# Planning durations of a recorded program order: measured instruction lengths and a length for mode changes

## The chip, the cores and the metric

One core of one Trainium2 chip runs the whole program. The metric is the device time of one execution in microseconds (us); less is better. TensorE does the matmuls, VectorE (DVE), ScalarE (ACT) and GpSimd (POOL) the rest, SyncE (SP) issues most DMAs. Each engine takes its instructions in the order of the program and waits, in place, for what each of them needs.

## What is computed

One layer of a hybrid decoder on 512 prompt tokens and 8 x 4 sample tokens, all fp32, followed by a norm. Cut to what matters:

```python
h = rmsnorm(x, p['norm1_g'])
z = h @ p['w_in']                              # 1024 -> 74 * 128 columns
uz, vz, sz, qz, gz = _split(z, (D_A, D_A, P_SHIFT, D_C, N_BRANCH * D_MODEL))
vn = layernorm(jax.nn.gelu(vz), p['ln_v_g'], p['ln_v_b'])
y_a = u * spatial_gate(vn, p['sg_w'], p['sg_b'])
y_b, wkv_new = rwkv7_branch(rz, kz, vbz, wl, al, gl, wkv_prev, p)   # a recurrence over tokens
y_c = memory_cross_attn(qz, mk, mv)
proj = jnp.einsum('nbtc,ncd->nbtd', branches, p['w_branch'])
x = x + jnp.einsum('nbtd,btnd->btd', proj, gates) @ p['w_out']
x = x + jnp.square(jax.nn.relu(rmsnorm(x, p['norm2_g']) @ p['w_up'])) @ p['w_down']
```

## The kernel before

**The trunk.** All weight products (`memk`, `memv`, `win`, `br`, `wout`, `up`, `down`) run in `trunk` (L500). Tokens are the 544 moving columns, in two halves of 256 and 288; a tile of 128 output columns takes 8 steps `kt`, and in each step three products of split operands (high x high, low x high, high x low, in the fast fp32 form), so 6 matmuls a step and 48 a tile. A tile of `win` is one of 74, so there are 3552 projection matmuls. A generator yields after each `kt`, so other streams can come between. Each half tile of weights (128 x 512) is loaded by SP, copied to its high part by ScalarE (L198, `whi`), and its low part is subtracted by VectorE (L211, `wlo`).

**The stages.** First the memory keys and values, beside the first norm. Then the RWKV stage, seven streams in order of priority: `chain_stream`, `inv_stream`, `fill_stream`, `prep_stream`, `out_stream`, `sample_stream`, and the trunk with `win`. Heads go in four groups of two pairs; `prep_pair` makes a pair's operands, `inv_stream` inverts triangular blocks (30 pairs of GpSimd instructions, L1010 and L1012, then a VectorE copy L1015), `fill` transposes (L977, copies L984 and L985), and `chain_stream` walks 16 chunks of 32 tokens, each step in three phases: matmuls C1 (L1067, L1069) and the copy Wt (L1072) with four scaled copies SP (L1077); C2 (L1083) with the copies Xo, Xe (L1086, L1087) and YU (L1090); C3 (L1094, L1096) with the additions into the next chunk's Xe, Xo (L1102). Each phase ends with `yield DONE`. `out_stream` norms a group's outputs (L1113 to L1127), transposes, adds and gates them (L1144 to L1158, gate product L543) and stores them in `yb_d`. `sample_stream` does the sample tokens (L1189 to L1295, state products L1221 and L1273).

Then the attention stage: `yb_stream` loads `yb_d` (L1371) and splits it into high and low parts (L1379, L1381), after which the trunk may do the 24 tiles of `br`, first those of the RWKV branch; `gate_in` transposes the gate input (L1415, L1416), `layer_norm`, `gate_out` (L1494) and the two attentions follow. The sample attention multiplies 16 cache blocks (L1560). The last branch's tiles wait for both attentions. Last the MLP, nearly all trunk.

**What sets the order.** `body` runs twice. In the dry run the engines are `ModelEngine`s: each call goes to `Model.op`, which keeps for each engine the time at which it is free, and for each tile when and by which engine it was written. `Sched.run` resumes the first stream in the list that is ready by TensorE's planned time, and records the pick. After `NOW` a stream is ready at once, after `DONE` when the last result of its piece is there plus 0.22 us (`m.done + GAP`), after `AFTER(t)` and `PAUSE(t)` some time later. PSUM slots (`take`) are recorded too. The second run emits the instructions in the recorded order. No cost is in the program itself; it only sets who comes when. `SWITCH`, `tensor` and the durations in `op` are what the change touches.

Of the kernel before, what the change touches and what calls it, by code (L numbers as in the profile page):

```python
# [11 lines left out]
F32R = mybir.dt.float32r  # L12
AF = mybir.ActivationFunctionType
ALU = mybir.AluOpType
# [44 lines left out]
class Shape:  # L59


    def __init__(self, shape, dt, base=None):
        self.shape, self.dt = tuple(shape), dt
        self.base = base or self
        if base is None:
            self.wrote = (None, None, 0.0)
# [35 lines left out]
class Model:  # L102

    def __init__(self):
        self.free = {"pe": 0.0, "v": 0.0, "s": 0.0, "g": 0.0}
        self.piece, self.start, self.done, self.side = 0, 0.0, 0.0, False

    def begin(self, ready):  # L110
        self.piece += 1
        self.start = self.done = ready

    def op(self, eng, name, a, k):
        if name == "dma_start":
            if eng in ("g", "s"):
                self.free[eng] = max(self.free[eng], self.start) + (1.04 if eng == "g" else 0.1)
            return
        aps = [x for x in list(a) + list(k.values()) if isinstance(x, Shape)]
        n = max(math.prod(x.shape[1:]) for x in aps)  # L120
        out = k.get("out") or a[0]
        if eng == "pe":
            n = math.prod(out.shape[1:])
            r = 0.85e-3 if name == "transpose" else 0.424e-3 if aps[1].dt == F32R else 1.68e-3
            t = n * r
        elif eng == "g":
            t = 0.17 + n * 1.7e-3
        elif eng == "v":
            t = 0.07 + n / 960.0
        else:  # L130
            t = 0.06 + n / 1160.0
        b = max(self.free[eng], self.start)
        for x in aps:
            piece, by, at = x.base.wrote
            if piece == self.piece and by != eng:
                b = max(b, at + 0.2)
        self.free[eng] = b + t
        if not self.side:
            out.base.wrote = (self.piece, eng, b + t)
            self.done = max(self.done, b + t)  # L140


class ModelEngine:
# [201 lines left out]
def body(nc, tc, io, plan, dry, dbg=None):  # L345
# [92 lines left out]
    def affine(tl, pattern, op, base, mult):  # L438
        G.affine_select(out=tl, in_=tl, pattern=pattern, compare_op=op, fill=0.0, base=base, channel_multiplier=mult)
# [1580 lines left out]
```

## Time and profile before

| | us |
|---|---|
| median of 3 runs (1484.18 to 1491.03) | 1484.28 |
| the profiled execution | 1485.83 |
| its span, first to last instruction | 1484.1 |
| TensorE busy in the span | 1404.7 (95%) |
| VectorE, ScalarE, GpSimd busy | 908.4, 590.1, 395.8 |
| mean granted TensorE clock | 0.982 |

Times in the profile are microseconds from the span's start. L500 is line 500 of the kernel before; PE is TensorE, PEld its weight loads. A tile's buffer number is left out (`hh` stands for all eight). A matmul on plain fp32 operands shows as two records. "Granted clock" is the share of full speed (2.4 GHz) that the chip allowed TensorE; 0.5 is 1.2 GHz.

### The profile page before, as it was taken

The page shows a single profiled execution, that of the slowest core. Times are in us where ns is not written, and L with a number is a line of the kernel's source. Part 1 is how long each engine was busy: PE and PEld are TensorE (multiplying, and loading weights), DVE is VectorE, ACT ScalarE, POOL GpSimd, SP SyncE. Part 2 cuts the span into 40 slices and gives each one's busy share as a digit, 9 for nine tenths or more (in the row PEclk, how much of TensorE's full clock was granted, in tenths as well). Part 3 has the DMA queues.
Part 4 walks back from the last instruction along what each step waited for, and adds up shares of the span by engine and source line. Part 5 has one row for each costly group of instructions (what it writes and reads, how often), then busy time and mean ns, then how long its engine had stood idle before and what let it go on. Part 6 is the DMA issues. An engine that isn't in the chain of part 4 may idle for free.

```text
span 1484.1 us, 30949 instructions
## 1 busy us (share of the span) xinstructions
PE 1404.7 (95%) x12390; PEld 1303.5 (88%) x12390; DVE 908.4 (61%) x1586; ACT 590.1 (40%) x1476; POOL 395.8 (27%) x462
## 2 busy tenths in 40 slices
PE   7899998998999899999998999989999999999997
PEld 7899987887888788887888896769999999999996
DVE  5757777776878877577675753424664454444544
ACT  3434334555565365555434123212433423323222
POOL 5320191272106602730233430112100030120223
PEclk9899998999999999999999999999999999999998
DMA  6642221222322323243468657654423322323222
GB/s 210 176 139 82 91 72 63 70 67 75 108 73 65 104 83 98 78 146 109 130 198 280 224 170 240 200 193 125 138 86 93 93 86 86 94 83 95 87 86 83
DMA packets 101888, 177.43 MB, mean 120 GB/s; under 512 B 14928, under 2 KB 28496, under 8 KB 101744
## 3 DMA queue, kind: packets, MB, share of 16 engines
q1 hardware_dynamic: 99904, 172.06, 36.8%
q8 instruction: 98, 1.61, 0.5%
q0 software_dynamic: 640, 2.23, 0.4%
q10 hardware_dynamic: 1200, 1.16, 0.2%
q14 instruction: 46, 0.38, 0.1%
HBM read 147.89 MB, written 27.51 MB: 118 GB/s over the span
## 4 chain that ended last, share of the span: by engine, by line
PE 63%; DVE 7%; POOL 5%; DMA 3%; ACT 2%; issue 2%; SPq 1%; POOLq 0%; DVEq 0%; ACTq 0%
PE pst L500 51%; POOL Xinv L1012 2%; POOL Tt L1010 2%; PE psc L1083 1%; PE psc L1067 1%; DVE wlo L211 1%; PE psc L1094 1%; PE pst L1646 1%; PE pst L1679 1%; PE pst L543 1%; PE pst L1817 1%; DMA craw<-cv 1%; PE pst L923 1%; POOL gn_va L1126 1%; PE pst L1494 1%
## 5 line engine op out<-in xcount | busy, mean ns | idle before, releaser
L211 DVE TENSOR_TENSOR wlo<-wraw,whi 128x512 fp32r<-128x512 f32 x372 | 309.8, 851 | 54.3 <-ACT whi L198 51.7
L198 ACT CAST whi<-wraw 128x512 fp32r<-128x512 f32 x372 | 224.0, 618 | 175.1 <-PE pst L500 111.8
L500 PE MATMUL pst<-hh,whi 128*128 128x256 f32 (+1 forms) x1184 | 274.2, 313 | 9.1 <-DVE Em L985 4.5
L500 PE MATMUL pst<-hh,wlo 128*128 128x256 f32 (+1 forms) x1184 | 246.7, 290 | 2.3 <-DVE wlo L211 2.3
L500 PE MATMUL pst<-hl,whi 128*128 128x256 f32 (+1 forms) x1184 | 246.1, 289 | 0.0
L500 PEld LDWEIGHTS pst<-hh,whi 128*128 128x128 f32 x1184 | 188.4, 191 | 29.5 <-issue 10.2
L500 PEld LDWEIGHTS pst<-hh,wlo 128*128 128x128 f32 x1184 | 191.5, 190 | 2.7 <-DVE wlo L211 2.7
L500 PEld LDWEIGHTS pst<-hl,whi 128*128 128x128 f32 x1184 | 192.2, 191 | 0.0
L1785 POOL TENSOR_TENSOR x<-x,dn 128x544 f32<-128x544 f32 x24 | 41.7, 1737 | 292.8 <-DVE dn L1783 292.8
L500 PE MATMUL pst<-gh,whi 128*128 128x256 f32 (+1 forms) x512 | 106.2, 289 | 0.0
L500 PE MATMUL pst<-gl,whi 128*128 128x256 f32 (+1 forms) x512 | 105.5, 287 | 0.0
L500 PE MATMUL pst<-gh,wlo 128*128 128x256 f32 (+1 forms) x512 | 105.0, 287 | 0.0
L500 PE MATMUL pst<-y_h,whi 128*128 128x256 f32 (+1 forms) x384 | 83.7, 299 | 0.5 <-ACT y_h L1604 0.5
L500 PEld LDWEIGHTS pst<-gl,whi 128*128 128x128 f32 x512 | 82.7, 189 | 0.0
L1090 ACT COPY YU<-psc 32x64 f32<-32x64 f32 x256 | 51.9, 203 | 76.1 <-DVE Xe L1087 70.7
L500 PEld LDWEIGHTS pst<-gh,whi 128*128 128x128 f32 x512 | 81.9, 188 | 0.1
L500 PEld LDWEIGHTS pst<-gh,wlo 128*128 128x128 f32 x512 | 81.7, 188 | 0.0
L1010 POOL TENSOR_TENSOR Tt<-Xinv 128x30 f32<-128x30 f32 (+14 forms) x120 | 67.9, 566 | 45.9 <-DVE Xinv L1005 37.1
L500 PE MATMUL pst<-y_h,wlo 128*128 128x256 f32 (+1 forms) x384 | 79.6, 289 | 0.0
L500 PE MATMUL pst<-y_l,whi 128*128 128x256 f32 (+1 forms) x384 | 79.5, 288 | 0.0
L1012 POOL TENSOR_TENSOR Xinv<-Xinv,Tt 128x30 f32<-128x30 f32 (+14 forms) x120 | 75.2, 627 | 9.4
L500 PE MATMUL pst<-mh,whi 128*128 128x256 f32 (+1 forms) x256 | 66.4, 300 | 8.5 <-ACT whi L198 7.9
(399 smaller groups left out, 2913.0 us busy)
## 6 DMA issues: line engine op xcount, KB each, us to landing
wraw<-win SPq DMA_DIRECT2D x148, 256.0 KB, 2.9
wraw<-up SPq DMA_DIRECT2D x64, 256.0 KB, 2.9
wraw<-down SPq DMA_DIRECT2D x64, 256.0 KB, 2.9
wraw<-br SPq DMA_DIRECT2D x48, 256.0 KB, 3.4
craw<-ck SPq DMA_DIRECT2D x16, 512.0 KB, 5.4
craw<-cv SPq DMA_DIRECT2D x16, 512.0 KB, 4.5
gz_d<-gzs SPq DMA_DIRECT2D x24, 272.0 KB, 3.0
gt<-gz_d SPq DMA_DIRECT2D x24, 272.0 KB, 2.9
```

The costliest lines, as they stand in the source:

```text
L198: self.nc.scalar.copy(hi, raw)
L211: (self.nc.gpsimd if pool else self.nc.vector).tensor_tensor(lo, raw, hi, op=ALU.subtract)
L500: PE.matmul(ps[:, o:o + n], lhsT=w[:, c], rhs=x[kt][:, s:s + n], start=kt == 0 and i == 0, stop=kt == KT - 1 and i == 2)
L543: PE.matmul(ps[:, o:o + n], lhsT=lhsT, rhs=rhs[:, s:s + n], start=True, stop=True)
L923: PE.matmul(ps[64:128, o:o + 64], lhsT=BK[0:64, c, :], rhs=A2[0][0:64, pi, c, :], start=True, stop=True, tile_position=(0, 64))
L1010: G.tensor_tensor(t3, X[:, j + 1:32, j:j + 1].to_broadcast([128, n, j]), X[:, j:j + 1, 0:j].to_broadcast([128, n, j]), op=ALU.mult)
L1012: G.tensor_tensor(X[:, j + 1:32, 0:j], X[:, j + 1:32, 0:j], t3, op=ALU.add)
L1067: PE.matmul(ps[64:128, pi * 64:pi * 64 + 64], lhsT=Ae[0:96, pi, c, :], rhs=Xe[0:96, pi, c, :], start=True, stop=True, tile_position=(0, 64))
L1083: PE.matmul(ps[q:q + 64, pi * 64:pi * 64 + 64], lhsT=CT[q:q + 64, m, :], rhs=Wt[q:q + 64, pi, :], start=True, stop=True, tile_position=(q, q))
L1090: S.copy(YU[q + 32 * pi:q + 32 * pi + 32, c, :], p3[q:q + 32, pi, :])
L1094: PE.matmul(ps[0:64, pi * 64:pi * 64 + 64], lhsT=Em[64:128, pi, c, :], rhs=Xe[64:128, pi, c, :], start=True, stop=True, tile_position=(64, 0))
L1785: G.tensor_tensor(x1[j], x1[j], t, op=ALU.add)
```

## The change

The model's durations are replaced: each kind of instruction gets one of its own (a scaled copy on ScalarE 0.1 us more, a power on GpSimd 0.4 us and more, slower shared stretches of VectorE and GpSimd), the delay from a write to its reader on another engine is 0.27 us from TensorE and 0.12 us from others where it was 0.2 us, and TensorE's matmuls go through `tensor`, which knows three modes (r: fast fp32, the trunk; f: plain fp32; t: parts of the array) and adds `SWITCH` where the mode changes. Nothing else is edited. Lines behind it stand 36 further on in the changed kernel.

```diff
--- before.py
+++ after.py
@@ -103,13 +103,32 @@
 
 
 
+
     def __init__(self):
         self.free = {"pe": 0.0, "v": 0.0, "s": 0.0, "g": 0.0}
         self.piece, self.start, self.done, self.side = 0, 0.0, 0.0, False
+        self.mode = "r"
 
     def begin(self, ready):
         self.piece += 1
         self.start = self.done = ready
+
+    def tensor(self, name, out, aps, tiled):
+
+        n, m = math.prod(out.shape[1:]), math.prod(aps[1].shape[1:])
+        if name == "transpose":
+            t, mode = 0.109 * max(1.0, n / 128), "f"
+        elif aps[1].dt == F32R:
+            t, mode = 0.0125 + n / 2400, "r"
+        elif tiled:
+            at_once = 4 if m <= 32 and aps[1].shape[0] == 128 else 2
+            t, mode = 2 * (0.003 + n / (850 if aps[1].shape[0] == 64 and m == 128 else 1200)) / at_once, "t"
+        else:
+            t, mode = 2 * max(0.112, 0.0025 + n / 1200), "f"
+        if mode != self.mode:
+            t += SWITCH[self.mode + mode]
+            self.mode = mode
+        return t
 
     def op(self, eng, name, a, k):
         if name == "dma_start":
@@ -119,25 +138,42 @@
         aps = [x for x in list(a) + list(k.values()) if isinstance(x, Shape)]
         n = max(math.prod(x.shape[1:]) for x in aps)
         out = k.get("out") or a[0]
-        if eng == "pe":
-            n = math.prod(out.shape[1:])
-            r = 0.85e-3 if name == "transpose" else 0.424e-3 if aps[1].dt == F32R else 1.68e-3
-            t = n * r
-        elif eng == "g":
-            t = 0.17 + n * 1.7e-3
-        elif eng == "v":
-            t = 0.07 + n / 960.0
-        else:
-            t = 0.06 + n / 1160.0
         b = max(self.free[eng], self.start)
         for x in aps:
             piece, by, at = x.base.wrote
             if piece == self.piece and by != eng:
-                b = max(b, at + 0.2)
+                b = max(b, at + (0.27 if by == "pe" else 0.12))
+        if eng == "pe":
+            t = self.tensor(name, out, aps, "tile_position" in k or aps[1].shape[0] == 64)
+        elif eng == "g":
+            if k.get("op") == ALU.pow:
+                t = 0.4 + n * 0.17
+            elif name == "memset":
+                t = 0.09 + n * 0.9e-3
+            else:
+                t = 0.18 + n * (2.3e-3 if self.free["v"] > b else 1.7e-3)
+        elif eng == "v":
+            if name in ("memset", "tensor_scalar"):
+                t = 0.155 + n / 1920
+            elif name == "reciprocal":
+                t = 0.15 + n / 160
+            elif name == "tensor_tensor_scan":
+                t = 0.1 + n / 480
+            elif name == "transpose":
+                t = 0.17 + n / (960 if n < 1024 else 560)
+            else:
+                t = 0.155 + n / 960 * (1.25 if n >= 500 and self.free["g"] > b else 1.0)
+        else:
+            scaled = sum(isinstance(k.get(x), Shape) for x in ("scale", "bias"))
+            t = 0.17 + 0.1 * scaled + n / 1200
         self.free[eng] = b + t
         if not self.side:
             out.base.wrote = (self.piece, eng, b + t)
             self.done = max(self.done, b + t)
+
+
+
+SWITCH = {"rf": 0.0, "fr": 0.11, "rt": 0.09, "tr": 0.2, "ft": 0.1, "tf": 0.11}
 
 
 class ModelEngine:
```

The instructions are the same; their order is not. At TensorE before, at the end of the RWKV stage (the first four rows are phase C3 of a late chain step, L500 the trunk, L1273 a sample state product):

```order
L1094 MATMUL psc<-Xe,Em 64x64
L1096 MATMUL psc<-Xo,Em 64x64
L1094 MATMUL psc<-Xe,Em 64x64
L1096 MATMUL psc<-Xo,Em 64x64
L500 MATMUL pst<-hh_93,whi 128x256
L500 MATMUL pst<-hh_93,whi 128x288
L500 MATMUL pst<-hl_101,whi 128x256
L500 MATMUL pst<-hl_101,whi 128x288
L500 MATMUL pst<-hh_93,wlo 128x256
L500 MATMUL pst<-hh_93,wlo 128x288
L1273 MATMUL pst<-ux,Ebd 128x512
L1067 MATMUL psc<-Xe,AG1e 64x64
```

Now, at the same place (L1119 is C2, L1130 and L1132 C3, L1309 the state product, L579 the gate product of the last two pairs, L1451 a gate input's transposes; the trunk's line is L536):

```order
L1309 MATMUL pst<-ux,Ebd 128x512
L1119 MATMUL psc<-Wt,CT_1028 64x64 x4
L1130 MATMUL psc<-Xe,Em 64x64
L1132 MATMUL psc<-Xo,Em 64x64
L1130 MATMUL psc<-Xe,Em 64x64
L1132 MATMUL psc<-Xo,Em 64x64
L1309 MATMUL pst<-ux,Ebd 128x512 x2
L579 MATMUL pst<-lg,wg_10107 128x256
L579 MATMUL pst<-lg,wg_10107 128x288
L579 MATMUL pst<-lg,wg_10124 128x256
L579 MATMUL pst<-lg,wg_10124 128x288
L1451 MATMUL pst<-ident,gv 128x128 x4
```

Trunk rows stood between the phases and between the state products; now none stands between them, or between them and what follows.

At VectorE before, at the end of the first inversion (L1015 is the copy that follows it, L904 and L905 make a half of the operands AG of the next pair, L211 the weights' low part):

```order
L725 SCALAR_TENSOR_TENSOR t_v<-pst,vec,t_v 128x511
L727 SCALAR_TENSOR_TENSOR t_v<-pst,vec,t_v 128x8x3
L728 SCALAR_TENSOR_TENSOR t_v<-sst,vec,t_v 128x8
L211 TENSOR_TENSOR wlo<-wraw,whi 128x512
L1015 COPY Xinv<-qmask 128x32
L904 TENSOR_TENSOR AG1o<-t_r,PP 64x16x32
L905 SCALAR_TENSOR_TENSOR AG1o<-t_L,PP 64x16x32
L1017 STREAM_TRANSPOSE Tt<-Xinv 128x32x32
L211 TENSOR_TENSOR wlo<-wraw,whi 128x512
```

Now, at the same place (L1051 is that copy, L940 and L941 the operands AG, L247 the low part):

```order
L247 TENSOR_TENSOR wlo<-wraw,whi 128x512
L1051 COPY Xinv<-qmask 128x32
L940 TENSOR_TENSOR AG1e<-t_r,PP 64x16x32
L941 SCALAR_TENSOR_TENSOR AG1e<-t_L,PP 64x16x32
L1053 STREAM_TRANSPOSE Tt<-Xinv 128x32x32
L247 TENSOR_TENSOR wlo<-wraw,whi 128x512
L940 TENSOR_TENSOR AG1o<-t_r,PP 64x16x32
L941 SCALAR_TENSOR_TENSOR AG1o<-t_L,PP 64x16x32
```

The copy behind the inversion now stands ahead of both halves AG1e and AG1o, where it stood between them.

## Rows read from the trace of the kernel before

**Rows 1.** Windows by stage: us, then busy us of each engine, clock, DMA share, GB/s
```profile
105.00:740.00 635.00, 602.37 (x6216) 536.55 (x6216) 466.40 (x946) 329.31 (x984) 212.35 (x291) 0.98 0.28 89
...
812.00:988.00 176.00, 163.50 (x1235) 135.77 (x1233) 85.44 (x138) 41.56 (x96) 41.77 (x26) 0.98 0.63 209
988.00:1484.10 496.10, 485.15 (x3873) 484.05 (x3873) 242.66 (x325) 153.82 (x271) 76.89 (x54) 0.99 0.31 95
```

**Rows 2.** Chain that ended last, whole run: start us, us, what
```profile
230.94 3.09 PE pst L500 x12
245.17 1.70 PE pst L500 x12
...
1091.68 364.60 PE pst L500 x2922
```

**Rows 3.** TensorE's waits, 105 to 740 us: total us, times, longest
```profile
PE psc L1094 <- DVE Xe L1087: 5.2, 5, 2.9
PE pst L500 <- DVE Em L985: 4.5, 4, 1.4
PE psc L1067 <- DVE Xe L1102: 4.2, 4, 2.6
PE pst L925 <- DVE AG1o L905: 3.9, 1, 3.9
```

**Rows 4.** VectorE's waits, 105 to 740 us: one pair
```profile
DVE Xinv L1015 <- POOL Xinv L1012: 12.0, 4, 6.6
```

**Rows 5.** Windows, as rows 1: a stretch behind a wait; the crossing
```profile
225.00:236.00 11.00, 8.94 (x153) 8.33 (x154) 8.31 (x10) 1.99 (x4) 0.81 (x3) 0.53 0.23 74
...
739.40:812.00 72.60, 66.64 (x480) 62.73 (x479) 48.46 (x75) 25.16 (x52) 20.25 (x27) 0.98 0.75 251
```

**Rows 6.** Groups by form, 105 to 740 us: count, busy us, mean ns, idle before
```profile
L500 PE MATMUL pst<-hh,whi 128*128 128x256 f32 x500 | 165.4, 331 | 6.7 <-DVE Em L985 4.5 <-ACT CT L1029 1.3 <-DVE t_vb L914 0.9
...
L500 PE MATMUL pst<-hl,whi 128*128 128x256 f32 x500 | 140.7, 281 | 0.0
...
L1077 ACT ACTIVATE SP<-Xe,PC 64x64 f32<-64x64 f32 x120 | 35.3, 343 | 0.0
...
L1072 ACT COPY Wt<-psc 128x128 f32<-128x128 f32 x64 | 17.0, 266 | 54.3 <-PE psc L1069 53.7
...
L1102 DVE TENSOR_TENSOR Xe<-psc,SP 64x128 f32<-64x128 f32 x56 | 15.7, 281 | 22.6 <-PE psc L1096 19.8 <-ACT YU L1090 1.9
```

**Rows 7.** Chain that ended last, the crossing
```profile
741.87 0.86 PE pst L1273 x2
...
757.49 0.70 DVE y_f L1144
...
766.14 2.89 DMA yb_d<-y_f
```

**Rows 8.** VectorE in time: end of the chain (738 to 756), last split (788 to 800)
```profile
739.56 0.61 DVE L1102 TENSOR_TENSOR SF<-psc,SP 64x128 f32<-64x128 f32 x2 [1.67 <-ACT whi L198]
...
798.81 0.72 DVE L1381 TENSOR_TENSOR y_l<-ybs,y_h 128x544 fp32r<-128x544 f32 x1 [0.34 <-ACT y_h L1379]
```

**Rows 9.** GpSimd in time, the crossing: start us, us, instruction, idle before
```profile
749.08 2.90 POOL L1126 TENSOR_TENSOR gn_va<-gn_va,mhalf 128x16 f32<-128x16 f32 x1 [2.03 <-DVE gn_va L1124]
752.06 1.90 POOL L1127 TENSOR_TENSOR YU<-YU,gn_va 128x1024 f32<-128x1024 f32 x1
...
772.91 1.29 POOL L1152 TENSOR_TENSOR y_f<-y_f,vbr 128x512 f32<-128x512 f32 x1 [11.73 <-ACT y_f L1150]
782.21 1.31 POOL L1371 DMA_DIRECT2D ybs<-yb_d  x2 [8.02 <-DMA yb_d<-ysT]
```

**Rows 10.** The page, costliest groups: the inversion
```profile
L1010 POOL TENSOR_TENSOR Tt<-Xinv 128x30 f32<-128x30 f32 (+14 forms) x120 | 67.9, 566 | 45.9 <-DVE Xinv L1005 37.1
...
L1012 POOL TENSOR_TENSOR Xinv<-Xinv,Tt 128x30 f32<-128x30 f32 (+14 forms) x120 | 75.2, 627 | 9.4
```

**Rows 11.** TensorE's waits, 812 to 988 us: one pair
```profile
PE pst L1494 <- POOL sgw L439: 2.0, 1, 2.0
```

## The prediction

> **What bounds the kernel now.** I read the windows by stage first. TensorE is busy in 602.37 of the 635 us of the RWKV stage (105 to 740 us), in 163.50 of the 176 us from the first branch matmul on (812 to 988), and in 485.15 of 496.10 us behind that [rows 1]. So the kernel is a queue of TensorE work, and a change of order can only move idle time: that ahead of 105 us (where the first projection matmul waits for the first norm), some 33 us in the RWKV stage, 6 in the crossing to the branches, 12.5 in the attention stage. A dense trunk matmul costs 364.60 / 2922 = 0.125 us [rows 2].
>
> The waits of TensorE in the RWKV stage [rows 3] show who makes the 33 us: VectorE late with Xe (5.2 and 4.2 us) and with Em (4.5), the copies behind the fill transposes. VectorE itself was held four times, 12.0 us, by the triangular inversion on GpSimd [rows 4]. Then I read the crossing, 739.4 to 812 us: TensorE is busy in 66.64 of 72.60 us [rows 5], although the work there is a long dependent chain on other engines. Trunk matmuls cover it: after the last chain step the order of before still has 402 of the 3552 projection matmuls (counted in the order), 50 us of cover at 0.125. That cover is what the change touches.
>
> **The change part by part.** No instruction is added or removed; only the recorded picks, slots and placements differ. The number of TensorE's mode changes, counted in both orders, is 596 before and 596 now. Tile to trunk goes from 169 to 191, other fp32 to trunk from 97 to 81, tile to other fp32 from 39 to 26. Coming back to the trunk costs: the first matmul of a group means 331 ns where the like one in mid-group means 281 [rows 6], 50 ns over 500 matmuls, 25 us in all, some 0.1 us for each return. Twenty-odd returns of a dearer kind against thirty cheaper ones: 0 to 4 us, I take **+2**.
>
> *Chain spacing.* In a chain step Wt is copied in 266 ns, then four scaled copies SP of 343 ns follow on ScalarE [rows 6]. The second phase needs Wt alone, but the stream says DONE behind all five, and the planner resumes it after the last. The old costs made SP 0.115 us each, the new ones 0.32; so the planner now wants 18 trunk matmuls between phases one and two: counted over 64 steps, 18 stand there 32 times instead of 4 (12 stood there 41 times). Sixteen steps now stretch over 580 to 610 trunk matmuls where they took 410 to 520. At the end the difference falls due: in the order of before the last chain step has 402 projection matmuls behind it; now **none**. The projection runs out with 13 phases still to come, and the sample states, the last two gate products and all 40 gate-input transposes stand bare.
>
> *The bare phases.* Without filling a phase lasts about its copies (266 ns of Wt; two of Xe and Xo, two additions of 281 [rows 6]) with 0.5 us for the matmuls and hand-overs on either side: 1.0 to 1.3 us, so 13 take about 16 us. TensorE's work in them is about 11 us (six state products of 0.86 [rows 7], 13 chain groups at about half of one of those). Idle **+5**, bounds 2 and 10.
>
> *The bare crossing.* From the last state addition (739.56) to the last low part of the first branch input (end of 799.53) the chain takes 60 us [rows 8]. In it the group norm's last GpSimd steps take 2.90 and 1.90 us, and the loads of the branch input wait from 753.96 to 782.21 [rows 9]. Between 753.96 and 774.20 lie two pairs; each needs four transposes of 0.70, an addition of 1.29 and a like time for the rest, about 5.6 us, with a store of 2.89 between them [rows 7, 9]: 14 us of the 20. The other 6, and 2 more ahead of the norm, are VectorE work that trunk and samples bring; they leave with the trunk. So the crossing takes 52 us. TensorE's own work in it: 66.64 less 50 for the trunk, less some 7 that now stand earlier or later, 9 us. It idles 43 us instead of 6: **+37**, bounds 26 (a chain of 41 us) and 45 (all 60).
>
> *The clock.* After the 3.9 us wait for AG1o, at 221 us [rows 3], the granted clock was 0.53 from 225 to 236 us, the lower level for nearly all of it [rows 5], and twelve trunk matmuls took 3.09 us instead of 1.70 [rows 2]. The crossing will end the same way: **+3**, bounds 0 and 11. The Trainium skill, "TensorE: Matmul & The Clock Gate", section "HAM oscillation — how this bites in real kernels", says the same against this change: work that follows each long wait starts at half rate. By that the crossing's own TensorE work would all run at the lower level too, and the sum would be 8 us higher.
>
> *Waits inside the stage.* The better VectorE and TensorE costs spread the fills (the eight fill transposes of group 0 now stand over 144 trunk matmuls instead of 120), and chain phases have more room. I take 12 of the 33 us away, **-12**. Bounds: all 33, and nothing. I don't take more because the inversion stays under-costed: its 60 GpSimd instructions last (67.9 + 75.2) / 4 = 35.8 us [rows 10] where the new costs make 28 to 34 of them, and the copy that waits for them still stands 7 to 9 low-part subtractions behind the start, as before; in group 0 it even stands ahead of both AG pairs now. The 3.9 us wait for AG1o [rows 3] came from just that queue.
>
> *Attention stage.* The gate products now start 252 branch matmuls after the first instead of 204, so the 2.0 us wait for sgw [rows 11] goes: **-2**. The end of the stage is as before: branch work runs out with five cache products left in both orders. The MLP's order is the same but for three matmuls at the end. Stage 0 waits for its norm in either order: 0.
>
> Sum: 37 + 5 + 2 + 3 - 12 - 2 = +33 on the profiled 1485.83 us; that execution stands 1.55 above the median of 1484.28, so **1517 us**.
>
> **The rivals.**
> *The inversion holds more.* The copy behind it comes up sooner on VectorE, and weights' low parts queue behind it. If each of the four holds VectorE for its worst 6.6 us [rows 4] instead of 3.0, TensorE loses the most of 14 us and nothing is saved: 1517 + 12 + 12 = 1541 at worst, about 1532. For it: the place in group 0. Against: new costs add 1 to 6 us to the planned inversion.
> *A cold crossing.* The lower clock holds through the crossing, its 9 us double and the first branch matmuls run at half: 1517 + 8 = 1525, with a longer chain 1530. For it: the stretch at 0.53 [rows 5].
> *No change.* All 33 us of RWKV waits vanish while the crossing costs what I say: 1517 - 21 = 1496, and with the crossing at its lower bound 1485.
> *Faster.* The waits vanish in both planned stages, 33 + 12.5 us, and the inversion's with them, by costs that now fit the chip. Then 37 + 5 + 2 + 3 - 45.5 is +1.5; it is faster than before once the crossing idles under 34 us too, e.g. 28: 1476. Against it: what VectorE waits for is GpSimd and DMA, whose costs stay low.
>
> **How the numbers follow.** About 0.5%, 7.4 us, is what a measurement of this kernel can tell from no change. Forecast (1496 to 1525) 0.66; inversion 0.12; cold crossing 0.10; no change 0.08; faster 0.04. Slower by over 0.5% is the first three, 0.88; the same 0.08; faster 0.04. The range takes the forecast and most of the two dearer cases: 1494 to 1536.
>
> **What would show it.** In the profile after: projection matmuls end before the chain; TensorE under half busy for some 45 us ahead of the first branch matmul, at a granted clock well under 1; the mean C1-to-C2 distance longer, with fewer waits for Xe and Em; DVE Xinv waiting 10 us or more for GpSimd in all; the stretch from the first branch matmul to the end within 8 us of before's 672. The prediction is wrong if that bare stretch is under 25 us long, or if TensorE's waits in the RWKV stage fall by more than 30 us.

## The result: 1.6% slower, and the profile after

The changed kernel takes 1510.03 us (median of four runs, 1509.75 to 1510.31), the kernel before 1485.38 in the runs beside it: a ratio of 1.0158, 95% interval 1.0131 to 1.0185. The forecast was 1517 us, slower. The profiled execution of the changed kernel has a span of 1508.0 us against 1484.1 and a mean granted clock of 0.972 against 0.982. In its code everything behind the planner stands 36 lines lower: the trunk matmul L500 is L536, the state product L1273 is L1309, the inversion L1010/L1012 is L1046/L1048.

The windows of the changed kernel, cut where the same pieces of work end as in [rows 1, 5] (the last chain phase now ends at 791 us, the first branch matmul starts at 840.08):

```profile
105.00:740.00 635.00, 609.99 (x6129) 553.25 (x6127) 452.55 (x898) 318.92 (x927) 198.05 (x282) 0.99 0.30 93
740.00:791.00 51.00, 43.21 (x476) 31.39 (x476) 30.63 (x64) 21.58 (x77) 12.37 (x11) 0.87 0.30 97
791.00:840.00 49.00, 16.13 (x59) 10.36 (x60) 26.09 (x42) 11.40 (x28) 15.36 (x21) 0.57 0.55 179
840.00:1011.00 171.00, 164.44 (x1256) 138.71 (x1253) 92.76 (x147) 42.07 (x97) 43.38 (x28) 0.98 0.65 223
1011.00:1508.00 497.00, 485.73 (x3875) 484.45 (x3873) 243.21 (x326) 154.00 (x271) 77.02 (x54) 0.99 0.31 95
```

Read as idle time of TensorE (the stretch less its busy time) against [rows 1, 5], this is the whole difference. To 740 us 25.0 idle instead of 32.6, so 7.6 won. From there to the first branch matmul 7.8 + 32.9 = 40.7 instead of 6.0, so 34.7 lost. The branch stage 6.6 instead of 12.5, so 5.9 won. The rest 11.3 instead of 11.0; ahead of 105 us 17.6 instead of 17.3. Sum +21.8, and 2.1 more busy time (1406.84 instead of 1404.72): +23.9, which is 1508.0 less 1484.1.

What TensorE waits for between 740 and 850 us (total us, times, longest):

```profile
PE pst L579 <- DMA wg<-wg: 18.8, 2, 10.3
PE pst L1451 <- DMA gv<-zv_d: 13.2, 5, 7.7
PE psc L1130 <- DVE Xe L1123: 3.2, 4, 0.8
```

These are the two gate products and the transposes of the gate inputs, on an engine that has no projection matmul left: the last of those ends at 766.2 us. The named DMAs are only what ended last. The work ahead of them is the group norm and the store, the chain of [rows 8, 9]: SyncE issues the loads of the gate inputs behind the stores of that chain. From SyncE's queue, VectorE and TensorE in time:

```profile
819.47 0.32 SPq L1196 DMA_DIRECT2D yb_d<-y_f  x1
821.07 0.93 SPq L1440 DMA_DIRECT2D gv<-zv_d  x2
...
793.33 0.60 DVE L1138 TENSOR_TENSOR SF<-psc,SP 64x128 f32<-64x128 f32 x2
828.99 0.72 DVE L1417 TENSOR_TENSOR y_l<-ybs,y_h 128x544 fp32r<-128x544 f32 x1 [9.21 <-ACT y_h L1415]
840.00 0.72 DVE L1417 TENSOR_TENSOR y_l<-ybs,y_h 128x544 fp32r<-128x544 f32 x1 [0.23 <-ACT y_h L1415]
...
839.13 1.09 PE L1451 MATMUL pst<-ident,gv 128*128 128x128 f32 x4 [0.73 <-DMA gv<-zv_d]
840.08 0.80 PE L536 MATMUL pst<-y_h,whi 128*128 128x256 f32 x2
```

The first low part (y_l) is ready at 829.7 us, the last at 840.72. The first branch matmul at 840.08 follows the last gate-input transposes without a gap, so two things end the crossing together: the last split and, on TensorE, the transposes that the order puts ahead of the branch work.

### The profile page after: what moved, and what is told of

Same layout as the page of the kernel before. It is cut to its first block, busy times and chain, and to the rows that moved or that the text cites. A ratio compares the mean times of both kernels' runs of the same rounds, so it can differ in the third digit from the quotient of the medians.

```text
span 1508.0 us, 30958 instructions
## 1 busy us (share of the span) xinstructions
PE 1406.8 (93%) x12390; PEld 1301.0 (86%) x12390; DVE 910.2 (60%) x1586; ACT 590.1 (39%) x1476; POOL 392.0 (26%) x462
## 3 DMA queue, kind: packets, MB, share of 16 engines
q1 hardware_dynamic: 99904, 172.06, 35.9%
## 4 chain that ended last, share of the span: by engine, by line
PE 70%; DVE 10%; POOL 8%; DMA 5%; issue 4%; ACT 2%; SPq 0%; POOLq 0%; DVEq 0%; ACTq 0%
PE pst L536 57%; POOL Xinv L1048 4%; POOL Tt L1046 3%; DVE wlo L247 2%; PE pst L1715 1%; PE psc L1103 1%; PE pst L1682 1%; PE psc L1119 1%; PE psc L1130 1%; PE pst L579 1%; PE pst L959 1%; PE pst L1853 1%; DVE y_f L1182 1%; DVE y_f L1180 1%; DMA lng<-lng 1%
## 5 line engine op out<-in xcount | busy, mean ns | idle before, releaser
L247 DVE TENSOR_TENSOR wlo<-wraw,whi 128x512 fp32r<-128x512 f32 x372 | 315.1, 864 | 45.6 <-ACT whi L234 43.0
L536 PE MATMUL pst<-hh,whi 128*128 128x256 f32 (+1 forms) x1184 | 271.8, 311 | 11.5 <-DVE Em L1021 7.4
L536 PE MATMUL pst<-hh,wlo 128*128 128x256 f32 (+1 forms) x1184 | 245.9, 289 | 5.7 <-DVE wlo L247 5.7
L536 PE MATMUL pst<-hl,whi 128*128 128x256 f32 (+1 forms) x1184 | 244.5, 288 | 0.0
L536 PEld LDWEIGHTS pst<-hh,whi 128*128 128x128 f32 x1184 | 186.4, 189 | 33.4 <-issue 8.8
L536 PEld LDWEIGHTS pst<-hh,wlo 128*128 128x128 f32 x1184 | 190.3, 189 | 6.2 <-DVE wlo L247 6.2
L536 PEld LDWEIGHTS pst<-hl,whi 128*128 128x128 f32 x1184 | 190.3, 189 | 0.0
L536 PE MATMUL pst<-gh,whi 128*128 128x256 f32 (+1 forms) x512 | 106.2, 289 | 0.0
L536 PE MATMUL pst<-gl,whi 128*128 128x256 f32 (+1 forms) x512 | 105.5, 287 | 0.0
L536 PE MATMUL pst<-gh,wlo 128*128 128x256 f32 (+1 forms) x512 | 105.1, 287 | 0.0
L536 PE MATMUL pst<-y_h,whi 128*128 128x256 f32 (+1 forms) x384 | 84.6, 301 | 0.5 <-ACT y_h L1640 0.5
L536 PEld LDWEIGHTS pst<-gl,whi 128*128 128x128 f32 x512 | 82.7, 189 | 0.0
L536 PEld LDWEIGHTS pst<-gh,whi 128*128 128x128 f32 x512 | 81.9, 188 | 0.1
L536 PEld LDWEIGHTS pst<-gh,wlo 128*128 128x128 f32 x512 | 81.8, 188 | 0.0
L536 PE MATMUL pst<-y_h,wlo 128*128 128x256 f32 (+1 forms) x384 | 79.7, 289 | 0.0
L536 PE MATMUL pst<-y_l,whi 128*128 128x256 f32 (+1 forms) x384 | 79.3, 288 | 0.0
L1046 POOL TENSOR_TENSOR Tt<-Xinv 128x30 f32<-128x30 f32 (+14 forms) x120 | 66.9, 557 | 47.1 <-DVE Xinv L1041 38.3
L536 PE MATMUL pst<-mh,whi 128*128 128x256 f32 (+1 forms) x256 | 65.7, 297 | 10.5 <-ACT whi L234 8.1
L1048 POOL TENSOR_TENSOR Xinv<-Xinv,Tt 128x30 f32<-128x30 f32 (+14 forms) x120 | 72.5, 604 | 9.4
```

The costliest lines, as they stand in the source:

```text
L247: (self.nc.gpsimd if pool else self.nc.vector).tensor_tensor(lo, raw, hi, op=ALU.subtract)
L536: PE.matmul(ps[:, o:o + n], lhsT=w[:, c], rhs=x[kt][:, s:s + n], start=kt == 0 and i == 0, stop=kt == KT - 1 and i == 2)
L1046: G.tensor_tensor(t3, X[:, j + 1:32, j:j + 1].to_broadcast([128, n, j]), X[:, j:j + 1, 0:j].to_broadcast([128, n, j]), op=ALU.mult)
L1048: G.tensor_tensor(X[:, j + 1:32, 0:j], X[:, j + 1:32, 0:j], t3, op=ALU.add)
```

## The experiments

The planner spends trunk matmuls ahead of each chain phase until its model says that the phase's inputs are there. So each plan is described by three means (trunk matmuls between phases one and two, two and three, three and the next one) and by how many projection matmuls it leaves behind the chain; both are counted in the order. My first theory, the **cover theory**, was the prediction's step: time goes with what is left behind the chain. Idle A is 635 us less TensorE's busy time in 105 to 740 us, idle B 110 less that in 740 to 850, both from the windows of each profiled run; busy is TensorE's busy time in the whole span, from the page of the run; the clock is the mean granted one. Each ratio is to the kernel before in the runs beside it, so ratios compare better between rows than medians do.

| run | trunk matmuls 1-2 / 2-3 / 3-1 | left | idle A | idle B | busy | clock | median us | ratio to before (95%) |
|---|---|---|---|---|---|---|---|---|
| before | 10.2 / 9.5 / 15.8 | 402 | 32.6 | 8.6 | 1404.7 | 0.982 | 1481.5 to 1485.4 | 1 |
| the change | 13.0 / 11.0 / 17.1 | 0 | 25.0 | 41.4 | 1406.8 | 0.972 | 1510.03 | 1.0158 (1.0131 to 1.0185) |
| olds | 9.8 / 10.9 / 18.8 | 120 | 25.7 | 23.7 | 1401.9 | 0.980 | 1492.04 | 1.0062 (1.0038 to 1.0086) |
| news | 16.3 / 12.8 / 12.3 | 0 | 27.9 | 33.5 | 1414.7 | 0.968 | 1516.03 | 1.0224 (1.0191 to 1.0257) |
| nosw | 12.1 / 11.9 / 16.3 | 0 | 18.5 | 49.6 | 1416.1 | 0.954 | 1527.93 | 1.0305 (1.0276 to 1.0334) |
| res8 | 10.7 / 9.3 / 15.1 | 384 | 41.3 | 15.1 | 1419.0 | 0.965 | 1510.12 | 1.0191 (1.0160 to 1.0222) |
| oldv | 13.8 / 11.2 / 11.9 | 348 | 47.3 | 10.4 | 1416.0 | 0.975 | 1508.28 | 1.0158 (1.0136 to 1.0180) |
| newp | 9.1 / 6.1 / 14.0 | 918 | 57.7 | 8.6 | 1421.3 | 0.967 | 1519.40 | 1.0224 (1.0188 to 1.0261) |
| newv | 8.9 / 10.7 / 19.6 | 0 | 16.7 | 42.3 | 1416.7 | 0.961 | 1516.12 | 1.0216 (1.0197 to 1.0235) |
| b_sp | 6.3 / 9.8 / 16.0 | 618 | 35.9 | 10.4 | 1408.7 | 0.981 | 1490.66 | 1.0047 (1.0027 to 1.0067) |
| a_spyu | 6.6 / 10.6 / 21.6 | 156 | 26.5 | 19.6 | 1407.7 | 0.977 | 1492.57 | 1.0053 (1.0035 to 1.0072) |
| spyu_res8 | 5.8 / 9.5 / 19.9 | 384 | 33.9 | 13.8 | 1413.5 | 0.973 | 1499.56 | 1.0099 (1.0083 to 1.0115) |
| spyu_v11 | 6.4 / 10.4 / 20.3 | 318 | 30.9 | 11.1 | 1411.1 | 0.975 | 1485.78 | 1.0003 (0.9989 to 1.0017) |
| spyug_v09 | 5.7 / 7.3 / 22.2 | 354 | 16.1 | 7.9 | 1398.8 | 0.988 | 1459.51 | 0.9834 (0.9814 to 0.9855) |

The two idle times are not the whole of a run's loss: with the same instructions TensorE is busy up to 16.6 us longer than before (newp) and 5.9 us shorter (spyug_v09). How much of that the lower clock makes, and how much the order itself, no run separates; where a theory below speaks of idle time, this part stays open.

**olds**: the change, with ScalarE's old cost.

```diff
-            scaled = sum(isinstance(k.get(x), Shape) for x in ("scale", "bias"))
-            t = 0.17 + 0.1 * scaled + n / 1200
+            t = 0.06 + n / 1160.0
```

> Changed kernel, with ScalarE's planning cost alone put back to 0.06 + n/1160 us. Its order leaves 120 projection matmuls (15 us at 0.125) behind the last chain step, against 0 in the change and 402 before; the 18s between phases one and two are gone (1 of 64). Cover theory (the loss is the crossing laid bare): 1510 less some 13 to 18 us, 1490 to 1498 us. Rival, mode costs (the loss comes from the planned time of TensorE's mode changes, which stay): 1505 to 1512. Rival, ScalarE alone (the longer DONE is all of it): 1482 to 1488.

Measured 1492.04: of the change's loss of 1.58%, 0.96 points (14 us) go with this one formula, 18 us by the medians (1510.03 to 1492.04), and idle B falls from 41.4 to 23.7.

**news**: the kernel before with the edit of olds turned round, nothing else.

> Kernel before, with the new ScalarE planning cost alone. Its order leaves no projection matmul behind the last chain step and one phase bare. Cover theory: the crossing is bare, 1500 to 1515 us. Rival, mode costs (not in this kernel): 1482 to 1488.

Measured 1516.03, 1 us above the range. ScalarE's true duration alone does the whole harm and a little more.

**nosw**: the change with all six entries of SWITCH at 0.

> Changed kernel, with all planned mode-change costs at zero. Cover stays 0 and 48 chain phases stand bare instead of 14. Cover theory: not faster than the change, 1508 to 1525 us. Rival, mode costs: 1484 to 1498.

Measured 1527.93, 3 us above the range: the durations for mode changes are a help inside this change, not its fault. The orders' own numbers of mode changes don't rank with the times: nosw has fewest (539, counted in the trace; before and the change 596, spyug_v09 627).

**res8**: the change, with the last 8 projection tiles held back until the last chain step.

```diff
-        put(1, always, ("win", col), ev_gelu(dst) if 8 <= i < 24 else ev_h(dst, fn, kw, flags))
+        put(1, always if i < 40 else lambda: "chain3" in sch.flags, ("win", col),
+        ev_gelu(dst) if 8 <= i < 24 else ev_h(dst, fn, kw, flags))
```

> Changed kernel, with its costs as they are, and the last 8 projection tiles (384 matmuls, 48 us) held back until the chain's last step is planned. All instructions and costs as in the change; only cover comes back. Cover theory: the crossing idles some 5 us instead of 43, and chain phases elsewhere lose 5 to 15 us by thinner filling: 1475 to 1490 us. Rival, spacing itself or mode costs make the loss: 1503 us or more.

Measured 1510.12, a clear miss. The crossing was covered again, but the held tiles were missing earlier. The windows of res8 from the point where other trunk work ran out:

```profile
680.00:700.00 20.00, 13.25 (x144) 9.67 (x144) 12.68 (x30) 9.24 (x34) 7.25 (x6) 0.66 0.35 97
700.00:720.00 20.00, 13.06 (x125) 6.78 (x122) 19.04 (x36) 9.52 (x39) 1.26 (x1) 1.00 0.42 128
720.00:740.00 20.00, 13.86 (x203) 10.95 (x199) 13.00 (x29) 6.37 (x25) 1.50 (x2) 0.58 0.02 9
740.00:764.00 24.00, 19.69 (x100) 9.04 (x100) 11.03 (x25) 8.04 (x32) 10.35 (x10) 0.50 0.31 101
764.00:777.00 13.00, 8.33 (x54) 4.45 (x56) 9.57 (x22) 4.60 (x19) 0.14 (x1) 0.50 0.29 99
777.00:812.00 35.00, 35.00 (x264) 34.57 (x265) 19.37 (x27) 12.24 (x26) 10.03 (x5) 0.94 0.44 140
```

From 680 to 777 us the chain runs bare, at half the clock at its end; from 777 on TensorE is full. The cover theory falls as I had it: the filling is finite, and keeping some for the end takes it from the chain. I replaced it by a padding theory (what a step takes in sum decides) and tested the other costs.

**oldv**: the change, with VectorE's old cost, `t = 0.07 + n / 960.0`.

> The change with VectorE's old cost, everything else as changed. 18 trunk matmuls stand between phases one and two 30 times, as in the change, but the chain has 348 projection matmuls behind it and no bare phase. Padding theory (what is lost is the trunk work that the planner spends ahead of the chain's end; the place of a pad does not matter, the sum over a step does): the sum per step is 36.9 trunk matmuls instead of 41.1, the chain ends about 768 us or earlier, time 1472 to 1490. Rival, that the 18s between phases one and two are what costs: as the run with ScalarE's cost alone, 1505 to 1520. Rival, that idle time only moves from the crossing into the chain (as in the run that held back eight tiles): 1500 to 1512, with 20 us of idle more between 423 and 740.

**newp**: the kernel before with the change's `tensor()` and SWITCH alone.

> The kernel before with the change's TensorE costs and mode changes alone. The plan has 918 projection matmuls behind the chain and only 29.2 trunk matmuls per chain step instead of 35.5; no cache product is left when the branch work runs out (5 before). Padding theory: TensorE's costs are the part of the change that helps; cover stays above the 350 that the crossing needs, so the crossing gives nothing back (6 us idle), the attention stage up to 10 us, and waits inside the chain grow by 0 to 15 us: 1470 to 1492. Rival, that chain steps of 29 trunk matmuls are too short for the chip (phase three waits for Xe, phase one for the additions): TensorE's waits in the RWKV stage double, 1495 to 1520.

Measured 1508.28 and 1519.40: the padding theory missed both, and both lie in ranges of the rivals. They have 348 and 918 projection matmuls left and a covered crossing (idle B 10.4 and 8.6), and lose inside the chain. TensorE's waits in 105 to 740 us, of oldv:

```profile
PE psc L1121 <- DVE Xe L1114: 10.1, 11, 3.1
PE pst L1053 <- DVE t_vb L941: 9.6, 1, 9.6
```

and of newp:

```profile
PE pst L1044 <- DVE t_vb L932: 9.8, 2, 8.6
PE psc L1112 <- DVE Xe L1105: 9.7, 14, 1.6
```

against 5.2 us for Xe in that phase and 0.9 for t_vb before [rows 3, 6]. In newp 6.1 trunk matmuls (0.76 us at 0.125) stand between phases two and three where 9.5 stood. In oldv it is 11.2, so the mean does not explain its waits. Of its 11, the one that ends at 395.73 us has this ahead of it on VectorE:

```profile
394.29 0.69 DVE L932 SCALAR_TENSOR_TENSOR AG0o<-t_L,PP 64x512 f32<-64x512 f32 x1
394.99 0.28 DVE L1113 COPY Xo<-psc 32x128 f32<-32x128 f32 x1
395.28 0.30 DVE L1114 COPY Xe<-psc 32x128 f32<-32x128 f32 x1
```

The copies queue behind other VectorE work that runs without a break; the old VectorE cost plans such work too short (0.20 us for a copy that takes 0.28). The rival that idle time only moves says 20 us more between 423 and 740 us: it is 5.5 (21.9 against 16.4), and 9.1 more ahead of 423. That the 18s are what costs is not excluded for oldv; newp and newv, with none and one of them in the order, lose as much without. The waits for t_vb are another matter, the inversion of the first group, which comes back in spyu_v11 below. From these runs I took a theory with **two sides**: too little between phases, and TensorE waits in the chain; too much, and the projection runs out ahead of the crossing. newv was the test of it.

**newv**: the kernel before with the change's VectorE costs alone.

> The kernel before with the change's VectorE costs alone. The plan takes 39.2 trunk matmuls per chain step (35.5 before), all of the rise between phase three and phase one and none of it by 18s; no projection matmul is left behind the chain and 19 phases stand bare. Two-sided theory (short steps make TensorE wait inside the chain, as with the TensorE costs alone; long steps use up the projection and leave the crossing bare, as with ScalarE's costs alone): slower like the other two parts alone, 1505 to 1522, with TensorE's idle time between 675 and 850 us at 50 to 75 us against 24 before and less than before's 68 us between 100 and 675. Rival, that only SP's cost and its 18s hurt: 1480 to 1495.

Measured 1516.12, as the two-sided theory said in kind: idle A is down to 16.7 and idle B up to 42.3. (The expectation's idle figures come from another count, of gaps between matmuls. By the windows TensorE idles 49.1 us between 675 and 850, against 9.0 before, and 9.8 between 105 and 675, against 32.2.) So the costs of ScalarE, VectorE and TensorE each alone make the kernel 2.2% slower, and the whole change 1.6%. GpSimd's durations and the new delays between engines were tried in no run by themselves.

**b_sp**: the kernel before; the four SP copies are planned as work that the next phase does not wait for.

```diff
+                    if dry:
+                        nc.model.side = True
                     for A, rows in ((Xe, slice(0, 64)), (Xo, slice(64, 128))):
...
+                    if dry:
+                        nc.model.side = False
```

> The kernel before with one planner edit: the four scaled copies SP are planned as work that the next phase does not wait for. Cover 618 instead of 402, C1 to C2 6.3 trunk matmuls instead of 10.2, two cache products left at the end of the branch work instead of 5. Padding theory: the crossing is covered either way; attention stage 4 to 8 us shorter; phase two waits for Wt a little more often (6.3 x 0.125 = 0.79 us of cover against a copy of 0.27 us and its hand-overs): 1472 to 1490. Rival, that the old wait for SP was what kept ScalarE's queue from delaying YU and Wt: 1490 to 1510.

Measured 1490.66: no gain, 0.5% slower, at the edge between the forecast and its rival. With 618 left instead of 402 idle B is no smaller (10.4 against 8.6), idle A rose by 3.3 us and the busy time by 4.0.

**a_spyu**: the change, with the same mark on SP and on the YU copies.

> The change with all its costs, but SP and the YU copies planned as work that the next phase does not wait for. 18s fall from 32 to 3, cover 156, no bare phase. Padding theory: between the run with ScalarE's old cost (cover 120, 1492) and before: 1482 to 1494. Rival, that ScalarE's cost hurts by other work than SP and YU (the weight parts, the gate values): as changed, 1505 to 1515.

Measured 1492.57, the time of olds. The true ScalarE cost stands in it, so that cost hurts by way of the plan, which lets phases two and three wait for copies that they don't read: without that wait it does no more harm than the old cost. SP and YU were marked together; which of the two counts for more is not shown.

**spyu_res8**: a_spyu with the tiles held as in res8. **spyu_v11**: a_spyu with VectorE's fixed part 0.11 instead of 0.155 us.

> The change with all its costs, SP and YU planned as work that the next phase does not wait for, and the last 8 projection tiles held until the chain is done: cover 384, 35.2 trunk matmuls per step, spread 5.8/9.5/19.9, three 18s. Two-sided theory: idle time in the crossing falls by 10 to 20 us against the run without the held tiles (1492.6), waits inside the chain rise by less, since steps of 35 are what the kernel before has: 1476 to 1490. Rival, that any held tile comes back as bare phases, as in the first run with held tiles (1510): 1492 to 1505.

> As the run with SP and YU not waited for, but VectorE's fixed part 0.11 us instead of 0.155: cover 318 instead of 156, 37.1 trunk matmuls per step (6.4/10.4/20.3) instead of 38.8, no bare phase, nothing held. Two-sided theory: half of the crossing's idle time goes (10 us), chain waits rise by 3 to 8 us: 1480 to 1492. Rival, that VectorE's shorter cost brings back its waits in full (as the run with its old cost, 1508, where C3 to C1 had 11.9): 1495 to 1508.

Measured 1499.56 and 1485.78. Holding tiles costs even here (the rival's range); shortening one cost by 0.045 us wins back the rest of the change's loss, as the two-sided theory said (idle B 8.5 us less than in a_spyu, idle A 4.4 more). It does so away from the truth: the copies Xo above take 0.28 us, about 0.155 + 128/960, so 0.11 is a value that suits the plan and not a better measurement. Steps of 35 with 384 left were no better than steps of 37 with 318 left, so neither number settles the time alone.

What was left in spyu_v11 was one wait in the first group. Its TensorE waits in 210 to 235 us begin with

```profile
PE pst L1062 <- DVE t_vb L950: 8.5, 1, 8.5
```

and VectorE in time shows why:

```profile
214.43 0.97 DVE L941 SCALAR_TENSOR_TENSOR AG1o<-t_L,PP 64x512 f32<-64x512 f32 x1
220.83 0.20 DVE L1051 COPY Xinv<-qmask 128x32 f32<-128x32 f32 x1 [5.43 <-POOL Xinv L1048]
222.21 2.00 DVE L1053 STREAM_TRANSPOSE Tt<-Xinv 128x1024 f32<-128x1024 f32 x1 [1.19 <-POOL Xinv L1048]
...
226.44 0.68 DVE L950 TENSOR_TENSOR t_vb<-t_v,pst 128x544 f32<-128x544 f32 x1
```

VectorE stands 5.43 us at the copy behind the inversion, and t_vb, for which TensorE waits, is queued behind it. The same copy holds VectorE for 6.6 us in oldv and 8.5 in newp, ahead of their waits for t_vb. The inversion takes longer than GpSimd's planned cost says [rows 10].

**spyug_v09**: as spyu_v11, and besides

```diff
-                t = 0.18 + n * (2.3e-3 if self.free["v"] > b else 1.7e-3)
+                t = 0.27 + n * (2.6e-3 if self.free["v"] > b else 2.0e-3)
...
-                t = 0.155 + n / 960 * (1.25 if n >= 500 and self.free["g"] > b else 1.0)
+                t = 0.09 + n / 960 * (1.25 if n >= 500 and self.free["g"] > b else 1.0)
```

> As the run with SP and YU not waited for and a shorter VectorE cost, and besides GpSimd's tensor operations at 0.27 us and 2.0 to 2.6 ns per element, so that the planned inversion lasts as long as the traced one; VectorE's fixed part 0.09 us brings the cover back to 354 with 35.2 trunk matmuls per step (5.7/7.3/22.2). Two-sided theory with the inversion as what is left: the one wait of 8.5 us at 218 us in the first group shrinks to under 3, crossing as well covered as before, 1472 to 1484. Rival, that what is won at the inversion comes back as waits for Xe between phases two and three (7.3 instead of 10.4): 1484 to 1495.

Measured 1459.51, 1.66% faster than the kernel before (1.45 to 1.86%) and below my range. The new formula makes 36 to 42 us of an inversion's 60 instructions, where 28 to 34 stood; the traced ones take (70.2 + 72.7) / 4 = 35.7. Who waited for the inversion, from its tile:

```profile
POOL Tt L1046: 34.0, 4
DVE Xinv L1051: 2.6, 1
```

VectorE waits 2.6 us for it instead of 12.0 [rows 4]. The windows of this run, with the stretch of the low clock as in [rows 5]:

```profile
225.00:236.00 11.00, 10.17 (x158) 9.55 (x158) 8.57 (x10) 2.80 (x6) 2.53 (x8) 1.00 0.30 100
...
105.00:740.00 635.00, 618.89 (x6377) 552.88 (x6377) 479.72 (x958) 335.02 (x998) 217.40 (x293) 1.00 0.29 92
...
740.00:850.00 110.00, 102.15 (x733) 94.55 (x731) 79.66 (x121) 33.39 (x69) 38.76 (x37) 0.98 0.70 237
```

The wait and the stretch at half clock behind it are gone, idle A is 16.1 and idle B 7.9: the one run that is good on both sides. The forecast reckoned with the wait and not with the busy time: against spyu_v11 TensorE idles 15.4 us less in the whole span and is busy 12.3 us less. Of the rival only a little came: the wait for Xe in phase three is 3.2 us instead of 1.5. Two numbers differ from spyu_v11 (GpSimd's cost and VectorE's 0.11 to 0.09), so how much each of them gives stays open.

## Why the prediction was right, step by step

**The direction and its mechanism** held. *Chain spacing*: the step said that ScalarE's true cost of SP, which the plan lets phase two wait for, pads each step and uses up the projection. news (ScalarE's cost alone, 1516) and a_spyu (the waiting for SP and YU taken away, 1492.57) show it. What the step did not see is that VectorE's and TensorE's costs each do as much harm alone, VectorE's by padding too, TensorE's with shorter steps and more left (918).

**The bare crossing** was mis-sized: +37 forecast, from 43 us idle. Its chain, from the last state addition (793.33) to the end of the last low part (840.72), took 47.4 us instead of 52, and TensorE was busy for 16.13 of the 49 us, not 9. Idle there is 32.9 us, 26.9 more than in the crossing before. So 7 of the 10 us by which the idle time was overrated are not time won: TensorE was busy in them, at the lower clock.

**The bare phases**: the trunk ran out at 766.2, and the chain's last phase ended 25.0 us later instead of 16. TensorE's work in that stretch was 17.2 us instead of 11. Idle of 7.8 in 740 to 791 lies inside the bounds of 2 to 10 for +5. Half of the stretch ran at the lower clock (third line; the first is a stretch behind a wait of 5.2 us, the last the crossing):

```profile
224.70:231.50 6.80, 4.56 (x24) 3.85 (x26) 6.75 (x9) 0.00 (x0) 0.00 (x0) 0.50 0.13 41
766.20:791.20 25.00, 17.21 (x124) 8.54 (x124) 13.01 (x30) 10.77 (x42) 10.95 (x10) 0.73 0.42 133
770.80:784.50 13.70, 10.46 (x51) 4.83 (x48) 6.33 (x14) 4.36 (x19) 6.08 (x6) 0.50 0.24 76
798.10:842.50 44.40, 16.27 (x56) 11.19 (x56) 22.61 (x40) 11.34 (x26) 13.56 (x21) 0.50 0.59 196
```

**The clock and mode changes**, +3 and +2 forecast: the rival of the cold crossing did happen, 0.50 (the 1.2 GHz level) from 798.1 to 842.5 us, through all but the first 7 us of the crossing and 2.4 us into the branches. A gate product and the transposes of a gate input, now and before:

```profile
801.83 2.15 PE L579 MATMUL pst<-lg,wg 128*128 128x256 f32 x4 [8.53 <-DMA wg<-wg]
824.12 1.08 PE L1451 MATMUL pst<-ident,gv 128*128 128x128 f32 x4 [7.74 <-DMA gv<-zv_d]
...
772.13 1.16 PE L543 MATMUL pst<-lg,wg 128*128 128x256 f32 x4 [0.92 <-DMA wg<-wg]
784.37 0.60 PE L1415 MATMUL pst<-ident,gv 128*128 128x128 f32 x4
```

In all the gate products are busy 4.30 us instead of 2.34, the 32 full transposes 8.45 instead of 5.25: 5.2 us more for the same work. Most of it lies under a chain on other engines. On the chain that ended last the transposes stand only from 827.40 to 829.78 us, so the low clock added perhaps 1 us there (an estimate, half of that stretch), and all busy time together rose by 2.1 us. The rule quoted from the Trainium skill ("TensorE: Matmul & The Clock Gate", "HAM oscillation — how this bites in real kernels") agrees with the low level behind the waits of 5.2 us (224.7 to 231.5) and of 8.5 to 10.3 us (the crossing); its 8 us did not add to the end. The low level from 770.8 us stands behind no long wait, only behind waits of 1.6 us and less after the trunk had run out. Mode changes in the order can't be a large cause: 596 in both, and coming back to the trunk costs what it did (327 ns against 281 now, 331 against 281 before [rows 6]):

```profile
L536 PE MATMUL pst<-hh,whi 128*128 128x256 f32 x592 | 193.3, 327 | 11.5 <-DVE Em L1021 7.4 <-DVE AG0e L973 1.1 <-DVE mkv L669 1.0
...
L536 PE MATMUL pst<-hl,whi 128*128 128x256 f32 x592 | 166.1, 281 | 0.0
```

Together the crossing, phases, clock and modes were forecast at +47 and came to 34.7 + 2.1 = 36.8.

**Waits inside the stage**: -12 forecast, -7.6 measured. TensorE's waits there, to be held against [rows 3]:

```profile
PE pst L536 <- DVE Em L1021: 7.4, 8, 2.5
PE pst L536 <- DVE wlo L247: 5.7, 2, 5.2
PE psc L1130 <- DVE Xe L1123: 3.2, 4, 1.5
PE psc L1103 <- DVE Xe L1138: 1.9, 2, 1.7
```

The waits for Xe fell from 9.4 to 5.1 us, as the forecast said of the longer spacing. Those for Em did not fall, against the forecast: 7.4 us in the trunk's row where 4.5 stood. The wait for AG1o at 221 us is gone and one of 5.2 us for a weight's low part stands in its place, behind the same inversion. VectorE in time:

```profile
222.26 0.20 DVE L1051 COPY Xinv<-qmask 128x32 f32<-128x32 f32 x1 [7.88 <-POOL Xinv L1048]
...
226.21 0.68 DVE L247 TENSOR_TENSOR wlo<-wraw,whi 128x512 fp32r<-128x512 f32 x1
```

So the rival that the inversion holds more came true in the first group, 7.88 us instead of 6.6 and with a low part queued behind it, but not in the sum: 10.4 us over the groups, 12.0 before. So the term was mis-sized by the fills (Em) and the inversion. That the inversion stays under-costed was the reason given for the small gain; spyug_v09, where its cost was raised (and VectorE's lowered), agrees with it.

**Attention stage**: -2 forecast, -5.9 measured. The wait for sgw [rows 11] is gone as said; the stage also has less idle time elsewhere.

The sum of the steps was +33 on the profiled execution; the profiled one after gave +23.9. The first four steps were 10.2 us too high, the stage's waits gave 4.4 less than forecast, the attention stage 3.9 more, and 0.6 more idle time came at the two ends. Errors of opposite sign cancelled in part, so that the time came out within 7 us is to that extent luck; the path was the one forecast. The forecast of the profile held: projection matmuls end before the chain, TensorE is busy a third of the time (16.13 of 49) ahead of the branches, at a clock of 0.57. The wait of VectorE for the inversion came to 10.4 us, as said; the stretch from the first branch matmul to the end is 668 us against 672.

## What to carry to other kernels

Better numbers in a planner's model are not better plans by themselves: here the durations of three engines, each alone, made the kernel 2.2% slower. For ScalarE the runs show why: its old error balanced a wait that the plan demanded and the program does not. For VectorE and TensorE no run shows what their old errors balanced. Correct what the plan waits for along with the durations, and look at both sides of the ledger, waits inside the chain and work left for the next dry stretch; a plan that moves idle time from one to the other (res8) wins nothing. What was left was found by the longest single wait in the trace, and behind it stood an operation whose planned length was still too short. The best plan here also holds one length, VectorE's 0.09 us, that is further from the measured one than the change's.

## What I had not expected

Where the bare work was the chain itself, a run lost more than its idle time. The span of nosw is 42.1 us longer than that of the kernel before: 30.8 us more idle (26.9 of them in the two windows, 68.1 against 41.2) and 11.4 us more busy time. Its window from 740 to 850 us ran at a granted clock of 0.63:

```profile
740.00:850.00 110.00, 60.37 (x487) 36.15 (x485) 61.62 (x123) 31.81 (x117) 28.62 (x33) 0.63 0.29 90
```

res8 shows the same, 13.0 us more idle and 14.3 us more busy time in a span 27.3 us longer, with its bare chain at 0.50 from 740 to 777. In the crossing of the changed kernel, where most of the chain is on other engines, the same low level cost little. How much of the added busy time is the clock's, and how much longer the clock made the chain's waits, these runs do not separate.
